# A softmax that streams 1 GB: loads cut into 48 KB and 16 KB per partition beside 64 KB stores

## The chip, the cores and the metric

The kernel runs on one core of a Trainium2 chip. The metric is device time in microseconds (us), the median of several runs; lower is better. The core's engines that matter here are VectorE (DVE in the profile), ScalarE (ACT), and SyncE (SP), which only issues transfers. Transfers between the chip's main memory and the on-chip buffer of 128 partitions are carried out by 16 DMA engines. Two queues feed them: SyncE's (q1 in the profile) and ScalarE's (q10).

## What is computed

A softmax over the last axis of a (16, 256, 32768) array of float32, with the temperature 1.0:

```python
def reference(logits, temperature):
    scaled = logits / temperature
    scaled = scaled - scaled.max(axis=-1, keepdims=True)
    exp_scaled = np.exp(scaled)
    return (exp_scaled / exp_scaled.sum(axis=-1, keepdims=True)).astype(np.float32)
```

Each of 4096 rows is cut into two halves of 16384 elements. A half lies in one partition, so that a tile is 128 halves (64 rows), 64 KB per partition, 8.39 MB. There are 64 tiles. Every byte is read once and written once: 536.87 MB each way.

## The kernel before

Three buffers of a tile each go round. A tile is loaded, then worked on in its buffer, then stored from the same buffer. Its work is: for each piece the negated maximum (VectorE) and the exponential with its sum (ScalarE); a short chain of small operations that joins the pieces and the two halves of a row and gives one factor per piece; and the scaling of each piece by its factor, shared between VectorE and ScalarE.

```python
_BUFS = 3
_LOAD = 16384                              # elements per partition in one load: 64 KB
_PIECES = (4096, 4096, 4096, 2048, 2048)   # pieces of a middle tile
_ON_DVE = (4096, 4096, 2048, 0, 0)         # of each, how much VectorE scales
_END = 4096                                # pieces, loads, stores of first and last tile
_END_ON_DVE = 2560
# ... cut ...
    def load(t):
        n = _END if t in (0, G - 1) else _LOAD
        for s in range(0, W, n):
            nc.sync.dma_start(out=buf[t % _BUFS][:, s : s + n],
                              in_=x[t * P : (t + 1) * P, s : s + n])

    def store(t, a, b):
        engine = nc.sync if t >= G - 2 else nc.scalar
        engine.dma_start(out=o[t * P : (t + 1) * P, a:b], in_=buf[t % _BUFS][:, a:b])
# ... cut ...
    def normalise(t):
        # ... cut: sizes, on_dve and at, the pieces' starts ...
        for k in range(K):
            xc = xs[:, at[k] : at[k] + sizes[k]]
            nc.vector.tensor_reduce(out=nm[:, k : k + 1], in_=xc, axis=X,
                                    op=A.max, negate=True)             # L101
            # ...
            nc.scalar.activation(out=xc, in_=xc, func=Exp, bias=nm[:, k : k + 1],
                                 scale=inv_t, accum_out=ssum[:, k : k + 1])   # L108
            if t == 1 and k == 0:
                store(0, 0, W)
        # ... cut: the small operations that give f, one factor per piece ...
        for k in range(K):
            a, b, c = at[k], at[k] + on_dve[k], at[k] + sizes[k]
            if b > a:
                nc.vector.tensor_scalar_mul(out=xs[:, a:b], in0=xs[:, a:b],
                                            scalar1=f[:, k : k + 1])   # L140
            if c > b:
                nc.scalar.activation(out=xs[:, b:c], in_=xs[:, b:c], func=Copy,
                                     scale=f[:, k : k + 1])            # L144
            if t == G - 1:
                store(t, a, c)
        if 0 < t < G - 1:
            store(t, 0, W)

    for t in range(_BUFS):
        load(t)
    for t in range(G):
        normalise(t)
        if t and t + _BUFS - 1 < G:
            load(t + _BUFS - 1)
```

Instructions start in this order on each engine and wait for the data that they need; a load waits until the store from its buffer is done. The stores of the last two tiles go out on SyncE's queue, behind the last load.

Of the kernel before, what the change touches and what calls it, by code (L numbers as in the profile page):

```python
# [1 line left out]

# [4 lines left out]


_SPLIT = 2
_BUFS = 3  # L10
_LOAD = 16384
_PIECES = (4096, 4096, 4096, 2048, 2048)
_ON_DVE = (4096, 4096, 2048, 0, 0)
_END = 4096
_END_ON_DVE = 2560
_SETS = 3


@with_exitstack
def kernel(  # L20
    ctx: ExitStack,
    tc: tile.TileContext,
    logits: bass.AP,
    temperature: bass.AP,
    out: bass.AP,
):
    nc = tc.nc
    inv_t = 1.0 / float(temperature)
    P = nc.NUM_PARTITIONS
    fp32 = mybir.dt.float32  # L30
    Exp = mybir.ActivationFunctionType.Exp
    Copy = mybir.ActivationFunctionType.Copy
    X = mybir.AxisListType.X
    A = mybir.AluOpType

    xf = logits.flatten_outer_dims()
    of = out.flatten_outer_dims()
    N, V = xf.shape
    W = V // _SPLIT
    assert sum(_PIECES) == W and len(_PIECES) == len(_ON_DVE)  # L40
    x = xf.rearrange("n (h v) -> (n h) v", h=_SPLIT)
    o = of.rearrange("n (h v) -> (n h) v", h=_SPLIT)
    G = N * _SPLIT // P
    assert G * P == N * _SPLIT
    n_rounds = _SPLIT.bit_length() - 1
    K = max(len(_PIECES), W // _END)

    pool = ctx.enter_context(tc.tile_pool(name="fixed", bufs=1))
    buf = [pool.tile([P, W], fp32, tag=f"x{b}", name=f"x{b}") for b in range(_BUFS)]
    widths = dict(nm=K, ssum=K, ee=K, f=K, ttj=K, nMh=2, Sh=2, rS=1)  # L50
    stat = [
        {
            k: pool.tile([P, w], fp32, tag=f"{k}{s}", name=f"{k}{s}")
            for k, w in widths.items()
        }
        for s in range(_SETS)
    ]

    def load(t: int) -> None:
        n = _END if t in (0, G - 1) else _LOAD  # L60
        for s in range(0, W, n):
            nc.sync.dma_start(  # L62
                out=buf[t % _BUFS][:, s : s + n],
                in_=x[t * P : (t + 1) * P, s : s + n],
            )

    def store(t: int, a: int, b: int) -> None:

        engine = nc.sync if t >= G - 2 else nc.scalar
        engine.dma_start(  # L70
            out=o[t * P : (t + 1) * P, a:b], in_=buf[t % _BUFS][:, a:b]
        )

    def combine(v, op) -> None:
        for j in range(n_rounds):
            mask = [i ^ (1 << j) for i in range(32)]
            nc.vector.stream_shuffle(  # L77
                out=v[:, j + 1 : j + 2], in_=v[:, j : j + 1], mask=mask
            )
            nc.vector.tensor_tensor(  # L80
                out=v[:, j + 1 : j + 2],
                in0=v[:, j : j + 1],
                in1=v[:, j + 1 : j + 2],
                op=op,
            )

    def normalise(t: int) -> None:
        xs = buf[t % _BUFS]
        if t in (0, G - 1):
            sizes = [_END] * (W // _END)  # L90
            on_dve = [_END_ON_DVE] * len(sizes)
        else:
            sizes, on_dve = _PIECES, _ON_DVE
        K = len(sizes)
        at = [sum(sizes[:k]) for k in range(K)]
        st = stat[t % _SETS]
        nm, ssum, ee, f, ttj = (st[k][:, :K] for k in ("nm", "ssum", "ee", "f", "ttj"))
        nMh, Sh, rS = st["nMh"], st["Sh"], st["rS"]
        for k in range(K):
            xc = xs[:, at[k] : at[k] + sizes[k]]  # L100
            nc.vector.tensor_reduce(  # L101
                out=nm[:, k : k + 1], in_=xc, axis=X, op=A.max, negate=True
            )
            if inv_t != 1.0:
                nc.vector.tensor_scalar_mul(
                    out=nm[:, k : k + 1], in0=nm[:, k : k + 1], scalar1=inv_t
                )
            nc.scalar.activation(  # L108
                out=xc,
                in_=xc,  # L110
                func=Exp,
                bias=nm[:, k : k + 1],
                scale=inv_t,
                accum_out=ssum[:, k : k + 1],
            )
            if t == 1 and k == 0:

                store(0, 0, W)
        nc.vector.tensor_reduce(out=nMh[:, 0:1], in_=nm, axis=X, op=A.min)  # L119
        combine(nMh, A.min)  # L120
        nc.scalar.activation(  # L121
            out=ee, in_=nm, func=Exp, bias=nMh[:, n_rounds : n_rounds + 1], scale=-1.0
        )
        nc.vector.tensor_tensor_reduce(  # L124
            out=ttj,
            in0=ee,
            in1=ssum,
            scale=1.0,
            scalar=0.0,
            op0=A.mult,  # L130
            op1=A.add,
            accum_out=Sh[:, 0:1],
        )
        combine(Sh, A.add)
        nc.vector.reciprocal(out=rS, in_=Sh[:, n_rounds : n_rounds + 1])  # L135
        nc.vector.tensor_scalar_mul(out=f, in0=ee, scalar1=rS)  # L136
# [3 lines that stand above are left out]
                nc.vector.tensor_scalar_mul(  # L140
                    out=xs[:, a:b], in0=xs[:, a:b], scalar1=f[:, k : k + 1]
                )
            if c > b:
                nc.scalar.activation(  # L144
                    out=xs[:, b:c], in_=xs[:, b:c], func=Copy, scale=f[:, k : k + 1]
# [6 lines that stand above are left out]
    with tc.manual_schedule():  # L152
# [8 lines that stand above are left out]
# [1 line left out]
_INS = ['logits', 'temperature']  # L162
_OUTS = [((16, 256, 32768), 'float32')]

_NUMBERS = {'temperature': 1.0}


# [26 lines left out]
```

## Time and profile before

| | |
|---|---|
| time, median of 3 runs | 2494.04 us (2493.56 to 2495.87) |
| maxima, VectorE (L101) | 318, 1117.5 us in all |
| exponentials, ScalarE (L108) | 318, 965.4 us in all |
| scaling on VectorE (L140), on ScalarE (L144) | 372.2 us, 370.9 us |
| VectorE waiting for loads | 683.8 us, 66 times |
| SyncE waiting for stores before it issues loads | 2382.1 us, 61 times |

The profile is that of one execution, of 2496.7 us. It names groups of instructions by the line of the kernel and the engine. Idle time of an engine that is not the bottleneck costs nothing, so the first question is which engine never idles; the DMA engines count as well. In the lines shown below, a digit in a row of 40 is the busy share of one fortieth of the span in tenths, where 9 is 90% or more. A queue's line gives its packets, megabytes and the time that its packets took as a share of 16 engines' span. A timeline line gives start, duration, engine, line and operation, the output and the input with their shapes, the count, and in brackets how long the engine sat idle before it and what ended that. A line of DMA issues ends with the median time from issue to landing.

### The profile page before, as it was taken

Reading aid. Unit: us, or ns where it says so; the run is one execution under the profiler, and the core shown is the slowest. Engines: PE = TensorE matmul, PEld = TensorE weight load, DVE = VectorE, ACT = ScalarE, POOL = GpSimd, SP = SyncE. Lnnn points to the kernel's source line nnn. Section 1 sums busy time; section 2 is a strip of 40 time slices with the busy share of each in tenths; the row PEclk is TensorE's granted clock in tenths of the full one; section 3 lists DMA queues with packets and bytes.
Section 4 is the critical chain, followed back from the end, with each engine's and each line's share of the span. In section 5 each row is a group of like instructions: output and inputs, shape, how many; then the busy total and the mean of one; then the engine's idle time right before and its main releaser. Section 6 shows DMA issues by size and latency. Waiting matters only on the chain.

```text
span 2496.7 us, 2616 instructions
## 1 busy us (share of the span) xinstructions
DVE 1575.6 (63%) x1216; ACT 1367.8 (55%) x895; POOL 0.2 (0%) x4
## 2 busy tenths in 40 slices
DVE  6576665766657656576565665656657566565665
ACT  6464654645546455464554645546455464554655
POOL 0000000000000000000000000000000000000000
DMA  9999999999999999999999999999999999999998
GB/s 419 436 429 430 433 437 436 435 437 426 434 434 437 433 426 435 434 436 423 433 433 433 435 425 436 436 433 425 435 422 436 421 437 436 421 436 422 436 429 380
DMA packets 19748, 1073.91 MB, mean 430 GB/s; under 512 B 2192, under 2 KB 2192, under 8 KB 2192
## 3 DMA queue, kind: packets, MB, share of 16 engines
q1 hardware_dynamic: 10800, 553.65, 51.4%
q10 hardware_dynamic: 8928, 520.10, 48.4%
q14 instruction: 20, 0.16, 0.0%
HBM read 536.87 MB, written 536.87 MB: 430 GB/s over the span
## 4 chain that ended last, share of the span: by engine, by line
DMA 73%; DVE 16%; ACT 9%; another core or an unknown queue 2%; issue 0%; SPq 0%; DVEq 0%; ACTq 0%
DMA x<-in_logits_dram 37%; DMA out_dram<-x 36%; DVE nm L101 12%; ACT x L108 7%; DVE x L140 3%; ACT x L144 2%; DVE f L136 0%; ACT ee L121 0%; DVE rS L135 0%; DVE Sh L80 0%; DVE ttj L124 0%; DVE Sh L77 0%; SPq L62 0%; DVEq L189 0%
## 5 line engine op out<-in xcount | busy, mean ns | idle before, releaser
L101 DVE TENSOR_REDUCE nm<-x 128x1 f32<-128x4096 f32 x318 | 1117.5, 3579 | 683.8 <-DMA x<-in_logits_dram 683.8
L108 ACT ACTIVATE x<-x,nm 128x4096 f32<-128x4096 f32 x318 | 965.4, 3036 | 1025.3 <-DVE nm L101 1025.3
L144 ACT ACTIVATE x<-x,f 128x2048 f32<-128x2048 f32 (+1 forms) x194 | 370.9, 1975 | 74.0 <-DVE f L136 74.0
L140 DVE TENSOR_SCALAR x<-x,f 128x4096 f32<-128x4096 f32 (+2 forms) x194 | 372.2, 1975 | 2.5 <-DVE f L136 0.2
L124 DVE CUSTOM_DVE_ANT_0 ttj<-ee,ssum 128x5 f32<-128x5 f32 (+1 forms) x64 | 10.6, 166 | 196.7 <-ACT ee L121 196.7
L108 ACT ACTIVATION_READ_ACCUMULATOR x<-x,nm 128x1 f32 x318 | 59.2, 186 | 0.0
L121 ACT ACTIVATE ee<-nm,nMh 128x5 f32<-128x5 f32 (+1 forms) x64 | 18.1, 284 | 0.0
L136 DVE TENSOR_SCALAR f<-ee,rS 128x5 f32<-128x5 f32 (+1 forms) x64 | 14.8, 231 | 2.2
L135 DVE RECIPROCAL rS<-Sh 128x1 f32<-128x1 f32 x64 | 10.5, 164 | 2.2
L80 DVE TENSOR_TENSOR Sh<-Sh 128x1 f32<-128x1 f32 x64 | 10.2, 159 | 2.2
L80 DVE TENSOR_TENSOR nMh<-nMh 128x1 f32<-128x1 f32 x64 | 10.2, 159 | 2.2
L119 DVE TENSOR_REDUCE nMh<-nm 128x1 f32<-128x5 f32 (+1 forms) x64 | 10.1, 158 | 2.2
L77 DVE STREAM_SHUFFLE Sh<-Sh 128x1 f32<-128x1 f32 x64 | 9.7, 151 | 0.0
L77 DVE STREAM_SHUFFLE nMh<-nMh 128x1 f32<-128x1 f32 x64 | 9.7, 151 | 0.0
L108 ACT ACT_TABLE_LOAD x1 | 1.3, 1283 | 8.1 <-DMA x<-in_logits_dram 8.1
L124 DVE DVE_READ_ACCUMULATOR2_ANT Sh<- 128x1 f32 x64 | 5.2, 82 | 0.0
L77 DVE LOAD_MASK_SELECT Sh<-Sh x64 | 0.9, 14 | 2.8
L77 DVE LOAD_MASK_SELECT nMh<-nMh x64 | 0.9, 14 | 2.8
L175 POOL MEMSET const-uint8-127<- 128x1 uint8 x1 | 0.1, 102 | 0.0
L175 POOL MEMSET const-bfloat16-1.0<- 128x1 bf16 x1 | 0.1, 101 | 0.0
L175 POOL MEMSET const-float32-0.0<- 128x1 f32 x1 | 0.1, 98 | 0.2 <-issue 0.2
L175 POOL MEMSET const-float32-1.0<- 128x1 f32 x1 | 0.1, 98 | 0.0
## 6 DMA issues: line engine op xcount, KB each, us to landing
x<-in_logits_dram SPq DMA_DIRECT2D x8, 2048.0 KB, 23.7
out_dram<-x SPq DMA_DIRECT2D x4, 2048.0 KB, 15.1
x<-in_logits_dram SPq DMA_DIRECT2D x62, 43.7
out_dram<-x ACTq DMA_DIRECT2D x62, 44.5
out_dram<-x SPq DMA_DIRECT2D x1, 29.4
```

The costliest lines, as they stand in the source:

```text
L77: nc.vector.stream_shuffle(out=v[:, j + 1 : j + 2], in_=v[:, j : j + 1], mask=mask)
L80: nc.vector.tensor_tensor(out=v[:, j + 1 : j + 2], in0=v[:, j : j + 1], in1=v[:, j + 1 : j + 2], op=op,)
L101: nc.vector.tensor_reduce(out=nm[:, k : k + 1], in_=xc, axis=X, op=A.max, negate=True)
L108: nc.scalar.activation(out=xc, in_=xc, func=Exp, bias=nm[:, k : k + 1], scale=inv_t, accum_out=ssum[:, k : k + 1],)
L119: nc.vector.tensor_reduce(out=nMh[:, 0:1], in_=nm, axis=X, op=A.min)
L121: nc.scalar.activation(out=ee, in_=nm, func=Exp, bias=nMh[:, n_rounds : n_rounds + 1], scale=-1.0)
L124: nc.vector.tensor_tensor_reduce(out=ttj, in0=ee, in1=ssum, scale=1.0, scalar=0.0, op0=A.mult, op1=A.add, accum_out=Sh[:, 0:1],)
L135: nc.vector.reciprocal(out=rS, in_=Sh[:, n_rounds : n_rounds + 1])
L136: nc.vector.tensor_scalar_mul(out=f, in0=ee, scalar1=rS)
L140: nc.vector.tensor_scalar_mul(out=xs[:, a:b], in0=xs[:, a:b], scalar1=f[:, k : k + 1])
L144: nc.scalar.activation(out=xs[:, b:c], in_=xs[:, b:c], func=Copy, scale=f[:, k : k + 1])
L175: nc = _bacc.Bacc("TRN2", target_bir_lowering=False, num_devices=1)
```

## The change

The load of a middle tile, one transfer of 64 KB per partition before, becomes two on the same queue: 48 KB (12288 elements, the first three pieces) and 16 KB (4096 elements, the last two pieces). The work on the first three pieces can then begin before the rest has landed, and a load's packets are no longer as large as those of the store that runs beside it on the second queue. Stores stay at 64 KB. The last tile is loaded, worked on and stored in pieces of 16, 16, 16, 8 and 8 KB instead of four of 16 KB, so that less is left to do after its last bytes land. The store of tile 0 is issued one piece later in the work on tile 1, since that work can now begin earlier.

```diff
-_LOAD = 16384
+_LOAD = (12288, 4096)
 _PIECES = (4096, 4096, 4096, 2048, 2048)
 _ON_DVE = (4096, 4096, 2048, 0, 0)
-_END = 4096
-_END_ON_DVE = 2560
+_FIRST_PIECES = (4096, 4096, 4096, 4096)
+_FIRST_ON_DVE = (2560, 2560, 2560, 2560)
+_LAST_PIECES = (4096, 4096, 4096, 2048, 2048)
+_LAST_ON_DVE = (2560, 2560, 2560, 2048, 0)
...
+    def cut(t: int) -> tuple:
+        if t == 0:
+            return _FIRST_PIECES, _FIRST_ON_DVE, _FIRST_PIECES
+        if t == G - 1:
+            return _LAST_PIECES, _LAST_ON_DVE, _LAST_PIECES
+        return _PIECES, _ON_DVE, _LOAD
+
     def load(t: int) -> None:
-        n = _END if t in (0, G - 1) else _LOAD
-        for s in range(0, W, n):
+        s = 0
+        for n in cut(t)[2]:
             nc.sync.dma_start(
                 out=buf[t % _BUFS][:, s : s + n],
                 in_=x[t * P : (t + 1) * P, s : s + n],
             )
+            s += n
...
-            if t == 1 and k == 0:
+            if t == 1 and k == 1:
 
                 store(0, 0, W)
```

More of the change, by code (lines that the diff above doesn't have):

```diff
@@ L45 @@
     n_rounds = _SPLIT.bit_length() - 1
-    K = max(len(_PIECES), W // _END)
+    K = max(len(_FIRST_PIECES), len(_PIECES), len(_LAST_PIECES))
     pool = ctx.enter_context(tc.tile_pool(name="fixed", bufs=1))
@@ L88, in normalise @@
         xs = buf[t % _BUFS]
[L89 to L93, printed above, removed]
+        sizes, on_dve, _ = cut(t)
         K = len(sizes)
```

## The prediction

> **What bounds the kernel now.** I read the page from the top. Its first two parts, with their figures by slice of time, and the list of DMA queues:
>
> ```profile
> span 2496.7 us, 2616 instructions
> DVE 1575.6 (63%) x1216; ACT 1367.8 (55%) x895; POOL 0.2 (0%) x4
> ...
> DMA  9999999999999999999999999999999999999998
> ...
> DMA packets 19748, 1073.91 MB, mean 430 GB/s; under 512 B 2192, under 2 KB 2192, under 8 KB 2192
> ...
> q1 hardware_dynamic: 10800, 553.65, 51.4%
> q10 hardware_dynamic: 8928, 520.10, 48.4%
> ```
>
> VectorE and ScalarE each idle for over a third of the span. The DMA digit is 9 in every slice but the last, and the two queues' packets fill 51.4 + 48.4 = 99.8% of 16 engines' span, some 2492 of 2496.7 us. That leaves about 5 us for the first bytes to arrive and the last to be confirmed. Nothing here waits for compute; the kernel is its 1073.7 MB, moved.
>
> The timeline on VectorE gives the speed at which they move. The first maximum of a tile starts when its data lands:
>
> ```profile
> 8.01 4.42 DVE L101 TENSOR_REDUCE nm<-x 128x1 f32<-128x4096 f32 x1 [8.01 <-DMA x<-in_logits_dram]
> 12.90 4.42 DVE L101 TENSOR_REDUCE nm<-x 128x1 f32<-128x4096 f32 x1 [0.47 <-DMA x<-in_logits_dram]
> 17.80 4.42 DVE L101 TENSOR_REDUCE nm<-x 128x1 f32<-128x4096 f32 x1 [0.47 <-DMA x<-in_logits_dram]
> 22.69 4.42 DVE L101 TENSOR_REDUCE nm<-x 128x1 f32<-128x4096 f32 x1 [0.48 <-DMA x<-in_logits_dram]
> ...
> 42.04 17.46 DVE L101 TENSOR_REDUCE nm<-x 128x1 f32<-128x4096 f32 x5 [3.88 <-DMA x<-in_logits_dram]
> ...
> 163.28 17.46 DVE L101 TENSOR_REDUCE nm<-x 128x1 f32<-128x4096 f32 x5 [8.98 <-DMA x<-in_logits_dram]
> ...
> 2418.69 17.46 DVE L101 TENSOR_REDUCE nm<-x 128x1 f32<-128x4096 f32 x5 [10.50 <-DMA x<-in_logits_dram]
> ```
>
> The four 16 KB pieces of tile 0 land (22.69 - 8.01) / 3 = 4.893 us apart, the 64 KB of tile 1 takes 42.04 - 22.69 = 19.35 us: 8.389 MB in 19.35 us is 433.5 GB/s, with loads alone. From tile 4 to tile 62 the period is (2418.69 - 163.28) / 58 = 38.886 us for one load and one store, 431.4 GB/s. Two directions beside each other are thus no faster than one, and 38.886 - 2 x 19.35 = 0.19 us a tile slower.
>
> The DMA issues say how the two queues share, and the landing of one store, from the same view in the stretch around 2408 us, says by what rule:
>
> ```profile
> x<-in_logits_dram SPq DMA_DIRECT2D x62, 43.7
> out_dram<-x ACTq DMA_DIRECT2D x62, 44.5
> ```
>
> ```profile
> L70 ACTq DMA_DIRECT2D out_dram<-x x1: 338/338/338, 2408.3 to 2408.3; - x1
> ...
> DMA to landing us min/median/max: 31.8/31.8/31.8
> ```
>
> Load 43.7, store 44.5 and the 28.05 us from a tile's landing (2418.69) to its store (issued at 2446.73 by the timeline) add to 116.2 us, three periods: the three buffers go round with no spare wait, each transfer stretched because it shares the engines. The store that leaves at 2408.3 meets the last tile's 16 KB load pieces instead of 64 KB, and lands in 31.8 us instead of 44.5.
>
> **What the skill says.** The page "DMA: Bandwidth & Descriptors", section "Queues, rings and completion order", says that each DMA engine takes turns between its queues packet by packet. The 31.8 us agrees: turn for turn, a 64 KB store packet loses less to a 16 KB packet. Its section "Where 436 GB/s comes from" puts the ceiling of the 16 engines at 435.2 GB/s; the measured 433.5 and 431.4 lie just below. An estimate from it: 1073.74 MB / 435.2 = 2467 us, plus the 5 us at the ends 2472, 0.9% under the time before. The section "Issuing engines are not separate DMA queues" says a second issuing queue brings no bandwidth, as the 431.4 beside 433.5 shows.
>
> **The change part by part.**
>
> *Middle loads in 48 + 16 KB.* Bytes are the same. A load of 128 partitions is 8 data packets and one closing packet on each of 16 engines (62 stores are the 8928 packets of q10: 144 each). Tile 0 is four transfers, 36 packets per engine, in 4 x 4.893 = 19.57 us; one whole load, 9 packets, takes 19.35. So a packet costs 0.22 / 27 = 8.2 ns beyond its bytes. The change adds 9 packets per engine to each of 62 loads: 62 x 9 x 8.2 ns = **+4.6 us**, on the path, since the engines have no gap to take it in.
>
> *What it does to the turns.* Per packet 64 KB take 19.35 / 8 = 2.42 us, 48 KB 1.82, 16 KB 0.61. Load and store no longer split the engines evenly: beside the 48 KB part a store gets 57%, beside the 16 KB part 80%. Stores finish early and then loads run alone. By hand, where it settles: the 48 KB part runs alone, 8 x 1.82 = 14.5 us after the tile before has landed; the 16 KB part meets the store, 8 x (2.42 + 0.61) = 24.2 us; together 38.8, a period, with no idle. It is consistent because VectorE takes the first three pieces (13.1 us) while the 16 KB part is still coming, so that from its landing to the store only about 14.5 us remain (two maxima 4.5, last exponential 2, the small combines 1.5 to 2, scaling 5.8), which is when the next 48 KB part is through. So the wait for data goes from one of 10 us a tile to one of about 11 us between pieces 2 and 3 and nearly none at piece 0. Compute still has slack, and it had slack before: **0 us**.
>
> *Does the load queue ever run dry?* Tile t+3's load leaves when store t is done, about when load t+1 has landed; load t+2 is then still to come, 38 us of work. So no.
>
> *Store 0 one piece later.* Tile 1's first 48 KB land at 22.69 + 14.5 = 37.2 instead of 42.04, VectorE is free at 38.2, and the second exponential is dispatched at 38.2 + 2 x 4.4 = 47; the store left at 46.50 before. **0 us**, and loads fill the engines until then.
>
> *Last tile in 16, 16, 16, 8, 8 KB.* Two transfers more, 18 packets per engine: **+0.15 us**. Whether compute is exposed at the end: store 62 and store 63 stand behind load 63 on one queue. Counted from the landing of tile 62, load 63 ends at 19.5, store 62 at 38.9. Tile 62 is ready at 14.5; tile 63's maxima take 17.5 more, its last exponential and combines 3 to 4, the first scaling 2: 37.5. The engines get their next bytes 1 us before they need them. Smaller last pieces bring the last part forward, but the transfers end the run: **0 us**.
>
> *The 0.19 us of mixing.* If it belongs only to time in which reads and writes alternate, 14.5 of 38.8 us would now be free of it: 62 x 0.19 x 0.37 = -4.4 us. It comes in jumps (periods of 38.5 to 40.0 us), and I don't know its cause; I count half, **-2 us**.
>
> Sum: 2494.0 + 4.6 + 0.15 - 2 = **2497 us**.
>
> **The rivals.**
> (a) *Calmer engines.* Uneven turns separate reads from writes, and all of the 0.19 us and some of the 5 us at the ends go: 4.6 - 12, about 2487. For it: the jumps are there with mixed traffic, and a load alone ran at 433.5. Against: the quick periods of 38.5 us have mixed traffic too.
> (b) *Starved loads.* The loads, with a fifth of the turns' bytes, come late, buffers come free late and the engines fall idle. It would be 1 or 2 us a tile, 2560 to 2620. Against it: an engine with one queue empty serves the other, and the load queue always holds a tile more; in the settled cycle nothing waits in a ring.
> (c) *The end exposed.* With stores ahead of loads no old store covers the last tile's compute; my margin is only 1 us. If the cycle settles elsewhere, so that load 62 lands late and load 63 close behind it, some 5 to 8 us are lost: 2503. For it: at the end of before, the last tile's first store left at 2470.9 while store 62 landed at 2446.7 + 29.4 = 2476.1, so the cover was only 5 us there as well.
>
> **Range and chances.** The sum's terms are of 5 us, so the difference should be within half a per cent: 2487 (rival a) to 2508 (c, and more jumps). Faster by 2% would be 2444 us, under the estimated floor of 2472: chance 0.01, for a ceiling that I misread. Slower by 2% needs (b): 0.03. Within 2%: 0.96.
>
> **What would show it.** In the changed kernel's profile: DMA packets 19748 + 62 x 144 + 288 = 28964; DMA digits still 9 everywhere; stores landing in about 26 us (24.2 and a confirmation) instead of 44.5; the two parts of a load about 51 and 76 us after issue, since they queue earlier; VectorE waiting for data about 128 times instead of 66, for about the same total of 680 us; the tile period 38.9 us, from the starts of the first maxima. Wrong would be: digits below 9 in the middle (b); a gap between the end of store 62 and the first store of 63 (c); a period under 38.7 us (a); or stores that still take 40 us, which would refute the turns.

## The result: 5.7% slower, and the profile after

The changed kernel takes 2632.7 us (median of 4 runs, 2630.51 to 2648.5) against 2494.36; the ratio is 1.0567, 95% interval 1.0526 to 1.0609. The predicted range ended at 2508.

The page of the changed kernel, the parts that answer to those of before: the span, the engines' busy time, the DMA share by fortieths of the span, the packets, and the queues (packets, MB, share of 16 engines).

```profile
span 2628.7 us, 2812 instructions
DVE 1580.5 (60%) x1217; ACT 1378.0 (52%) x897; POOL 0.2 (0%) x4
...
DMA  9999999999999999999999999999999999999997
...
DMA packets 28966, 1073.93 MB, mean 409 GB/s; under 512 B 3216, under 2 KB 3216, under 8 KB 3216
...
q1 hardware_dynamic: 20016, 553.66, 50.4%
q10 hardware_dynamic: 8928, 520.10, 47.5%
```

The digits still read 9, and by them alone nothing has happened. The queues' line tells more. Packets fill 97.9% of 2628.7 us, 2573.5 us, where before it was 99.8% of 2496.7, 2491.7 us. So of 132 us more, about 82 are the same bytes under way for longer, and about 50 are idle time of the DMA engines (55.2 us against 5.0). I call these **stretch** and **idle** below; both come from the printed shares, so they are good to about 3 us. VectorE and ScalarE work about as long as before.

The trace's records of single packets (no view prints them) say what stretch looks like. The median packet of each size takes what the prediction gave it: 2.42, 1.82 and 0.61 us. But 10.2% of the packets take over 5% longer than the median of their size, where it was 2.7% before.

The DMA issues, with the median time from issue to landing (the second line also holds the 7 pieces of 16 KB of the first and last tile):

```profile
x<-in_logits_dram SPq DMA_DIRECT2D x62, 6144.0 KB, 47.2
x<-in_logits_dram SPq DMA_DIRECT2D x69, 2048.0 KB, 60.2
...
out_dram<-x ACTq DMA_DIRECT2D x62, 37.1
```

Stores land in 37.1 us instead of 44.5, not in 26; the parts of a load in 47 and 60, not in 51 and 76. So the stores do gain by the turns, but by less than was worked out. VectorE's waits for loads, with their total, their number and the longest:

```profile
DVE nm L107 <- DMA x<-in_logits_dram: 866.5, 116, 22.1
```

About 128 waits and 680 us in all were expected.

VectorE's timeline shows what became of the steady rhythm. Between the first and the last line, these are successive waits for data; the tiles' first maxima (x3) and those of the 16 KB part (x2):

```profile
156.19 17.46 DVE L107 TENSOR_REDUCE nm<-x 128x1 f32<-128x4096 f32 x5 [0.83 <-DMA x<-in_logits_dram]
...
1684.01 13.07 DVE L107 TENSOR_REDUCE nm<-x 128x1 f32<-128x4096 f32 x3 [19.78 <-DMA x<-in_logits_dram]
...
1704.24 4.48 DVE L107 TENSOR_REDUCE nm<-x 128x1 f32<-128x2048 f32 x2 [7.17 <-DMA x<-in_logits_dram]
...
1719.80 13.07 DVE L107 TENSOR_REDUCE nm<-x 128x1 f32<-128x4096 f32 x3 [1.85 <-DMA x<-in_logits_dram]
...
1738.13 4.48 DVE L107 TENSOR_REDUCE nm<-x 128x1 f32<-128x2048 f32 x2 [5.26 <-DMA x<-in_logits_dram]
...
1767.12 13.07 DVE L107 TENSOR_REDUCE nm<-x 128x1 f32<-128x4096 f32 x3 [15.28 <-DMA x<-in_logits_dram]
...
2544.54 13.07 DVE L107 TENSOR_REDUCE nm<-x 128x1 f32<-128x4096 f32 x3 [1.34 <-DMA x<-in_logits_dram]
```

Tiles begin 35.8 us apart, then 47.3: they come in pairs. From tile 4 (156.19) to tile 62 (2544.54) long periods (42 to 51 us) and short ones (30 to 38 us) alternate without exception, and the mean is 2388.35 / 58 = 41.18 us, against 38.886.

The end of such a pair, in stretches of 2 us (columns: stretch, its length, busy time of VectorE, ScalarE and GpSimd, clock, DMA share, GB/s):

```profile
1744.00:1746.00 2.00, 0.88 (x7) 0.94 (x3) 0.00 (x0) 1.00 0.72 303
1746.00:1748.00 2.00, 1.97 (x1) 1.91 (x2) 0.00 (x0) 1.00 0.16 66
1748.00:1750.00 2.00, 2.00 (x2) 2.00 (x3) 0.00 (x0) 1.00 0.11 49
1750.00:1752.00 2.00, 1.84 (x2) 1.88 (x1) 0.00 (x0) 1.00 0.15 57
1752.00:1754.00 2.00, 0.00 (x0) 0.00 (x0) 0.00 (x0) 1.00 1.13 483
```

This view counts a packet whole in the stretch in which it starts, so a share can pass 1. Followed packet by packet in the trace, two of the 16 DMA engines are at work from 1748 to 1753 us, while VectorE and ScalarE scale the tile whose store leaves at 1751.93. A digit of the page averages 66 us and hides it. Before, between 200 and 2300 us, never fewer than 15 packets were under way.

Why a load that VectorE awaits until 1738.13 is late can be counted in the trace, which has one completion per engine for every transfer (no view prints them). Fourteen of the 16 engines had finished their part of that transfer 32 us before the last one, one 18 us before. The median span from a transfer's first completion to its last is 17 us in this run and 7 us before. It is a few engines that trail: between 150 and 2300 us, 11 of a load's 16 completions come within 1.4 us of the first (the median), the last one 28.9 us after it. A transfer is as late as its last engine.

### The profile page after: what moved, and what is told of

Same layout as the page of the kernel before. It is cut to its first block, busy times and chain, and to the rows that moved or that the text cites. A ratio compares the mean times of both kernels' runs of the same rounds, so it can differ in the third digit from the quotient of the medians.

```text
span 2628.7 us, 2812 instructions
## 1 busy us (share of the span) xinstructions
DVE 1580.5 (60%) x1217; ACT 1378.0 (52%) x897; POOL 0.2 (0%) x4
## 3 DMA queue, kind: packets, MB, share of 16 engines
q1 hardware_dynamic: 20016, 553.66, 50.4%
q10 hardware_dynamic: 8928, 520.10, 47.5%
## 4 chain that ended last, share of the span: by engine, by line
DMA 52%; DVE 23%; another core or an unknown queue 14%; ACT 8%; issue 2%; SPq 0%; ACTq 0%
DMA x<-in_logits_dram 28%; DMA out_dram<-x 23%; DVE nm L107 19%; ACT x L150 4%; ACT x L114 4%; DVE x L146 3%; DVE f L142 0%; ACT ee L127 0%; DVE rS L141 0%; DVE Sh L90 0%; DVE ttj L130 0%; DVE Sh L87 0%; SPq L71 0%; ACTq L195 0%
## 5 line engine op out<-in xcount | busy, mean ns | idle before, releaser
L90 DVE TENSOR_TENSOR nMh<-nMh 128x1 f32<-128x1 f32 x64 | 10.2, 160 | 2.2
L90 DVE TENSOR_TENSOR Sh<-Sh 128x1 f32<-128x1 f32 x64 | 10.2, 160 | 2.2
## 6 DMA issues: line engine op xcount, KB each, us to landing
out_dram<-x ACTq DMA_DIRECT2D x62, 37.1
```

The costliest lines, as they stand in the source:

```text
L90: nc.vector.tensor_tensor(out=v[:, j + 1 : j + 2], in0=v[:, j : j + 1], in1=v[:, j + 1 : j + 2], op=op,)
```

## The experiments

Theory at the start, **turns**: an engine that alternates between queues packet by packet gives unequal packets unequal shares; engines drift apart, and all else follows. Rivals: **pieces** (more, smaller transfers cost by themselves), **early start** (the work on a tile begins and its store leaves at another moment), and the **end** (last tile). The ratios are to the kernel before, run beside each, and leave out runs over 1.5% above the fastest of their kernel; for two kernels whose runs spread widely that would keep only the quicker half, so the runs themselves are given.

### Which part of the change

```diff
 cut_only: the changed kernel, but
-_LAST_PIECES = (4096, 4096, 4096, 2048, 2048)
+_LAST_PIECES = (4096, 4096, 4096, 4096)        # _LAST_ON_DVE: four times 2560
-            if t == 1 and k == 1:
+            if t == 1 and k == 0:
 last_only: the changed kernel, but
-_LOAD = (12288, 4096)
+_LOAD = (16384,)
```

> Only the loads of the middle tiles are cut (48 + 16 KB); last tile and the store of tile 0 are as before. All theories that put the loss in the middle expect 2625 to 2640 us, as with the whole change (2632.7). If the last tile or the later store of tile 0 carries part of it, 2600 or less.

> Only the last tile in smaller pieces and the store of tile 0 one piece later; middle loads whole. If the loss is in the middle: 2494 us, within 5. If the end carries part of it: over 2500.

Cut loads alone: 2633.53 us, ratio 1.0565 (1.0512 to 1.0617). Last tile and later store alone: 2496.7, ratio 1.0002 (0.9989 to 1.0015). All of the loss belongs to the cut of the middle loads; the rival of the end falls.

### Equal packets on both queues; a late start

```diff
 both_32: the changed kernel, but
-_LOAD = (12288, 4096)
+_LOAD = (8192, 8192)     # and the store of a middle tile in two of 8192 as well
 late_start: the changed kernel, but, for middle tiles, pieces are taken from the end:
+            at = [W - at[k] - sizes[k] for k in range(K)]
```

> Loads and stores of the middle tiles both in 32 + 32 KB: twice the transfers of the whole change's kind on both queues, but equal packets on both. Theory of turns (unequal packets let the 16 engines drift apart; equal packets don't): near before plus 124 x 9 packets x 8.2 ns = 9 us, so 2495 to 2510 us, and loads land in about the time that stores do. Rival of pieces (more and smaller transfers cost by themselves, or two transfers a tile let compute start early): as slow as the change or slower, 2600 to 2700 us.

> Loads 48 + 16 KB as in the change, but the work on a middle tile begins with the 16 KB part that lands last, so that nothing starts early. Theory of turns: still slow, 2600 to 2660 us. Rival of the early start (the store now leaves at another moment against the loads, and that costs): back near 2500 us.

Equal halves: the four runs took 2503.47, 2519.06, 2561.4 and 2561.88 us, too wide apart for a ratio, and on both sides of the 2510 us that the theory allowed. The profile is of the fastest (span 2501.6): the queues fill 99.8%, with some 5 us of stretch and 5 of idle, although the completions of a load there come 16 us apart (the median between 150 and 2300 us). What slowed the other two isn't shown. So smaller pieces are not slow by themselves, but equal packets are no sure cure. The late start: 2554.01, ratio 1.023 (1.021 to 1.025), between what both theories expected. Its queues:

```profile
q1 hardware_dynamic: 20016, 553.66, 51.5%
q10 hardware_dynamic: 8928, 520.10, 48.1%
```

99.6% of a span of 2551.2 us is 2541.0 us of packets: the idle time is nearly gone (10.2 us), of the 82 us of stretch 49 stay. And the engines finish closer together than before the change (3.0 us from first to last, the median). Stretch thus doesn't need transfers that end far apart.

### One queue

```diff
 one_queue_cut: the changed kernel, but
-        engine = nc.sync if t >= G - 2 else nc.scalar
+        engine = nc.sync
 one_queue_64: that, and
-_LOAD = (12288, 4096)
+_LOAD = (16384,)
```

> The whole change, but every store goes out on SyncE's queue behind the loads, so that no DMA engine has two queues to take turns between. Theory of turns: all 16 engines do the same packets in the same order, stay together, and the loss is gone: 2490 to 2515 us. Rival of the cut itself (an early start of the work, more packets): still 2550 to 2640 us.

> As the run before, with loads of 64 KB in one transfer. Theory of turns: near the kernel before, 2480 to 2505 us, and about 5 us (62 x 9 packets x 8.2 ns) below the cut loads on one queue. If one queue holds a load up behind a store that waits for compute, 2510 or more, with DMA digits below 9.

With the cut: 2495.88 us, ratio 0.9993 (0.9983 to 1.0002). Without: 2496.86, ratio 1.0001 (0.9984 to 1.0017). The same transfers, in the same sizes, with the same early start, cost nothing when all stand in one queue. Its page and VectorE's timeline:

```profile
span 2493.6 us, 2749 instructions
...
q1 hardware_dynamic: 28944, 1073.75, 99.7%
```

```profile
1011.65 17.46 DVE L107 TENSOR_REDUCE nm<-x 128x1 f32<-128x4096 f32 x5 [10.73 <-DMA x<-in_logits_dram]
1050.36 17.46 DVE L107 TENSOR_REDUCE nm<-x 128x1 f32<-128x4096 f32 x5 [10.73 <-DMA x<-in_logits_dram]
```

28944 packets, as many as the two queues of the changed kernel had (20016 + 8928). The period between these two lines is 38.71 us; from tile 4 to tile 62 the mean is 38.88, that of before. The wait between the two parts is gone as well: behind each other in one queue the 16 KB land within the 13 us in which VectorE takes the first three pieces. This rules out pieces and early start as causes on their own. The 5 us that more packets should cost didn't show either.

### Other sizes

```diff
 load_32:    _LOAD = (8192, 8192), stores 64 KB
 store_cut:  _LOAD = (16384,), stores of middle tiles in 12288 + 4096
 store_16:   _LOAD = (12288, 4096), stores in four of 4096
 load_16:    _LOAD = (4096, 4096, 4096, 4096), stores 64 KB
 load_16_48: _LOAD = (4096, 12288), stores 64 KB
 late_32:    load_32 with the late start
```

> Loads 32 + 32 KB beside stores of 64 KB on the second queue. Theory of turns: a load's packets are half of a store's in both parts, so the engines drift apart: 2540 to 2640 us. If only the small 16 KB part does it (a store packet four times as large): 2500 to 2530 us.

> Turned round: loads of 64 KB in one transfer, stores in 48 + 16 KB on the second queue. Work can't start early. Theory of turns in its simple form: unequal packets again, 2540 to 2640 us. Rival of the early start, and of loads that fall behind stores: the loads are now favoured, about 2500 us.

> Loads 48 + 16 KB and the early start as in the change, but stores of the middle tiles in four transfers of 16 KB, so that a load packet that takes turns waits 0.61 us for a store packet instead of 2.42. If slow loads beside large store packets are the cause: most of the loss gone, 2500 to 2530 us (27 more packets a tile and engine, 62 x 27 x 8.2 ns = 14 us, are in that). If the early start by itself, or packets of unequal size whichever way round, is the cause: 2560 us or more.

> Loads in four transfers of 16 KB beside stores of 64 KB: a load meets a store packet four times its own in every part. If the loss grows with the store packet against the load packet: slower than the change, 2640 to 2720 us. If two landings a tile are what counts: about 2600, as with 32 + 32.

> The two parts the other way round, 16 KB first and 48 KB second: the same packets, and the work can begin early on only the first of the five pieces, so the store leaves some 24 us after the landing instead of 15. If the moment of the store is what divides 2633 from 2554: near the late start, 2545 to 2590 us. If the packets alone count: 2620 to 2640.

> Loads 32 + 32 KB as in the run at 2608 us, with the work of a tile begun at the half that lands last. If the early start adds to the loss by moving the store to the moment when the next load is exposed to it: 2530 to 2570 us, as the late start did for 48 + 16. If it mattered only for the 16 KB part: unchanged, 2590 to 2620.

Stretch is the packets' time beyond the 2491.7 us of before; some 5 us of it (14 where something is cut in four, 18 in store_16) is the estimate for more packets. Stretch and idle are those of the one profiled execution, which for store_cut was slower than the median (2517.46 us).

| run | median us | ratio (95%) | stretch | idle |
|---|---|---|---|---|
| change | 2632.7 | 1.0567 (1.0526 to 1.0609) | 82 | 55 |
| load_32 | 2607.96 | 1.0441 (1.0417 to 1.0465) | 56 | 60 |
| store_cut | 2503.78 | 1.0039 (1.0017 to 1.0062) | 19 | 5 |
| store_16 | 2561.72 | 1.0221 (1.0154 to 1.0288) | 65 | 8 |
| load_16 | 2554.59 | 1.0196 (1.0133 to 1.0259) | 59 | 8 |
| load_16_48 | 2596.92 | 1.0363 (1.0297 to 1.0429) | 38 | 57 |
| late_32 | 2619.44 | 1.0451 (1.037 to 1.0533) | 80 | 42 |

For store_16 and load_16 the intervals reach from 1.3 to 2.9%: slower, by about 2%. Three expectations fell. Cut stores beside whole loads are just as unequal and lose 0.4%, so inequality is not enough; it matters which side is small. Loads of 16 KB meet the largest relative store packet and lose less than those of 32 KB, so the loss doesn't grow with that proportion. And the late start, which took half of the loss away at 48 + 16 KB, takes nothing away at 32 + 32. Two more runs settle less than they were meant to. Load_16_48 came out between its two expectations. And store_16 came out where slow loads beside large store packets are not the cause: its loads land in 25.5 and 28.0 us, sooner than before, its engines are idle for 8 us, and still 65 us of stretch are there.

### Transfers alone

What was open by then: whether stretch comes from the two queues alone or needs the work between load and store.

```diff
 copy_64, copy_cut, copy_32: loads of 64, of 48 + 16, of 32 + 32 KB, and no softmax;
 each tile is stored as it was loaded, so the output is the input
-            normalise(t)
+            store(t, 0, W)       # the last tile in its five pieces
 both_48_16: the changed kernel, with the stores of middle tiles in 12288 + 4096 too
```

> The softmax left out: every tile is stored as it was loaded, right after its landing; loads of 64 KB, stores of 64 KB on the second queue. The base for the next two: 2480 to 2500 us, DMA digits 9.

> As the run before, with loads in 48 + 16 KB. If unequal turns alone throw the engines out of step and stretch packets: 2530 to 2600 us, the queues' shares adding to nearly the whole span. If the work between load and store is needed for the loss: 2485 to 2510 us.

> As the run before, with loads in 32 + 32 KB: 2530 to 2600 us if turns alone do it, 2485 to 2510 us if the work is needed.

> With the softmax: loads and stores of the middle tiles both in 48 + 16 KB on their two queues. If it is the mean size of the packets on the two queues that must agree: 2500 to 2515 us. If the turns must be equal packet by packet, a 48 KB load part beside a 16 KB store part still disturbs: 2530 to 2600 us.

Without the work, 64 KB: 2500.63, ratio 1.0017 (0.9998 to 1.0036). 48 + 16 KB: 2514.92, ratio 1.0077 (1.0058 to 1.0096). 32 + 32 KB: 2612.54, ratio 1.044 (1.0375 to 1.0505), as much as with the softmax. The page of copy_64, then of copy_32:

```profile
span 2486.5 us, 307 instructions
...
q1 hardware_dynamic: 11088, 553.65, 51.6%
q10 hardware_dynamic: 8928, 520.10, 48.3%
```

```profile
span 2616.8 us, 372 instructions
...
q1 hardware_dynamic: 20016, 553.66, 51.1%
q10 hardware_dynamic: 8928, 520.10, 48.0%
```

99.9% of 2486.5 is 2484 us of packets, 99.1% of 2616.8 is 2593 us: the same bytes are under way for 109 us more, where nothing computes. (The first profile is of the quickest of 13 runs, the second of the slowest of four; the medians are 112 us apart.) So for 32 + 32 KB stretch is made by the transfers of two queues. For 48 + 16 KB, though, the transfers alone lose 0.8%, and only together with the softmax between load and store 5.7%. The page of copy_cut:

```profile
span 2522.5 us, 372 instructions
...
q1 hardware_dynamic: 20016, 553.66, 52.1%
q10 hardware_dynamic: 8928, 520.10, 47.8%
```

The queues fill 99.9%, so what it loses is stretch as well, without idle.

The packet records also tell whether loads and stores slow each other just by being under way at once. Count at each moment the packets under way of either queue and take the smaller number: between 200 and 2300 us it is 4.9 on average in copy_64 and 6.2 in both_32, but 2.3 in the changed kernel. Yet only 0.9% and 1.8% of the packets take over 5% longer than the median of their size there, against 10.2%. Mixing alone is not the cause.

With both queues cut 48 + 16 the 20 runs again spread, from 2496.13 to 2614.39 us with a median of 2542.08, over both of the ranges that were expected: this run decides nothing.

### The store's moment, and 32 + 32 KB on one queue

```diff
 late_store: the changed kernel; ahead of each middle tile's store on ScalarE
+            for s in (0, 4096, 8192):    # three copies in place, times 1.0
+                nc.scalar.activation(out=xs[:, s : s + 4096], in_=xs[:, s : s + 4096],
+                                     func=Copy, scale=1.0)
 one_queue_32: load_32 with every store on SyncE's queue
```

> The change with three copies of 4096 elements in place on ScalarE (3 x 3.7 us, times 1.0) ahead of each middle tile's store: work begins early, the store leaves about 26 us after the landing instead of 15. If the moment of the store makes the difference between 2633 and the late start's 2554: 2540 to 2580 us in spite of more work. If the early start of VectorE's work makes it, or spare time in the ring of buffers: 2630 us or more.

> Loads 32 + 32 KB, stores of 64 KB, all on SyncE's queue. If turns between two queues are needed for the loss: 2490 to 2505 us, against 2608 on two queues. If 32 KB packets are slow in themselves: 2590 or more.

Late store: 2622.12, ratio 1.0491 (1.0459 to 1.0522), between its two expectations but nearer to the second. Holding the store back doesn't do what the late start did, so its moment alone isn't what divides 2633 from 2554; the copies also lengthen the work on a tile, so the two runs differ in more than the store's moment. Its idle time is 65.6 us, more than the change's. A buffer held longer in work leaves less in the queues; that this is the reason is argued. One queue, 32 + 32: 2495.75, ratio 0.9991 (0.9972 to 1.001), where two queues took 2607.96.

## Why the prediction was wrong

**What bounds the kernel** held: the DMA queues fill 97.5 to 99.9% of the span in every run, compute has slack on average. (The 435.2 GB/s that the prediction takes from the Trainium skill, "DMA: Bandwidth & Descriptors", section "Where 436 GB/s comes from", is there the ceiling of the 16 ports into the on-chip buffer, not of the engines. The same section holds that main memory binds such transfers at about 358 GB/s; the 431.4 and 433.5 measured here go beyond that.) **The packet term**, +4.6 us, was of no matter; on one queue the cut loads show none of it in the time. **The last tile and store 0**, 0 us each: right (1.0002).

**The step that failed** is "What it does to the turns", with its "no idle" and "0 us", and after it "Does the load queue ever run dry? ... no". Two assumptions in it were wrong:

- I treated 16 engines as one, each packet with a fixed time (2.42, 1.82, 0.61 us) whatever else goes on. The median packet kept these times, but with cut loads beside the second queue 10.2% took over 5% longer, and the packets' time grew by 82 us. The profile before had held a trace of this in the 0.19 us a tile of mixing, which I took for a small term to be halved: from tile 4 to tile 62, what packets took there beyond the median of their size comes to 12 us of all 16 engines' time, 0.2 us a tile. The jumps of single periods up to 40.0 us are not explained by it: in the period of 40.0 us it is 0.4 us. Copy_32 shows that stretch needs no compute.
- The cycle I settled by hand was one load, one store, one tile of work per period. The kernel found another one, of two tiles. With tiles in pairs and loads that wait for their last engine, the buffers are at times all in work or held by a straggler, and the engines have nothing: 50 us more idle. One such pair is followed above; that all the idle time comes about like this is argued. Uneven starts alone don't make it: in the late start tiles begin in threes (28, 31 and 60 us apart), its engines finish together, and its idle time is 10 us. The queue's "38 us of work" that I counted was a mean over a regular rhythm.

Rival (b), engines that fall idle because loads come late, was nearest, at a chance of 0.03. Its "1 or 2 us a tile" came out as 2.3 (41.18 - 38.886), but its mechanism is only the smaller part of that, and its sign, DMA digits below 9 in the middle, would have missed it. Rivals (a) and (c) showed nowhere.

**What is shown and what is not.** Shown: the cut of the middle loads makes the loss, only beside a second queue, and not by pieces or an early start of their own. Shown for 32 + 32 KB: the transfers alone do it. Not shown: why packets stretch. That the turns set engines moving against each other is argued from the completions of the changed kernel; the late start, with engines that end together and 49 us of stretch, speaks against it as the whole story, and cut stores that lose 0.4% say that inequality alone is no measure. Completions that are far apart and stretch don't go together in the other runs either: 16 us and 5 us of stretch in both_32, 2.1 us (the loads) and 65 in store_16. Nor is it shown why 48 + 16 KB needs the softmax for most of its loss and 32 + 32 does not.

## What to carry to other kernels

Where two queues share the DMA engines at their ceiling, a steady alternation of whole, equal packets is worth keeping (equal ones that were cut had runs from 2496 to 2614 us); cutting the loads beside whole stores cost 2 to 6% here with the softmax between them, with no byte and no wait added. If transfers must be cut, try them on one queue first: that gave the time of before for both cuts that were tried. Read the queues' shares times the span, not the row of digits, to see whether a bound by DMA got slower packets or gaps; and when tiles start at unequal distances, take the mean period before trusting a schedule worked out by hand for one tile.

## What the runs showed of the hardware that I had not expected

- Two issuing queues can cost. The Trainium skill's "DMA: Bandwidth & Descriptors", section "Issuing engines are not separate DMA queues", says that a second one "will only save the time on the sequencer it takes to initiate the DMA". Here the equal 64 KB packets of two queues match one queue (1.0001), but with cut loads two took 2632.7 us and one 2495.88.
- An engine can lag most others of its transfer by 32 us, more than the 19.35 us that a whole 64 KB load took alone.
- The direction matters: with the softmax, small load packets beside 64 KB stores cost 2.0 to 5.7%, stores of 48 + 16 KB beside 64 KB loads 0.4%.
- A DMA-bound kernel can get slower by a minority of its packets: the median packet of each size took as long as before, and 10.2% instead of 2.7% took over 5% longer.
